# Column halves for the 128x64 products of a triangular inverse, ScalarE copies behind them, and fewer turns of waiting around it

## The chip, the cores and the metric

The kernel runs on one core of a Trainium2 chip. The metric is the time on the device in microseconds (us), the median over runs of the same program. The engines are TensorE (PE in the profile; its weight loads are PEld), VectorE (DVE), ScalarE (ACT), GpSimd (POOL) and SyncE (SP), which issues nearly all DMAs. PSUM has eight banks that TensorE writes and VectorE and ScalarE read.

## The reference

One block of a hybrid decoder, batch 1, 1024 tokens, model width 1024, in float32. After an RMSNorm one projection feeds two groups of heads: eight heads of stick-breaking attention (width 64) and four heads of gated DeltaNet (width 128). Both outputs are normed, gated, projected back and added to the residual; a last RMSNorm follows. What the change touches is the chunked delta rule. There each chunk needs the inverse of a unit lower triangular matrix:

```python
a_mat = jnp.where(strict, jnp.einsum('bhnid,bhnjd->bhnij', k_beta, k) * decay, 0.0)
eye = jnp.eye(CHUNK, dtype=jnp.float32)
rhs = jnp.concatenate([v_beta, k_beta * jnp.exp(g)[..., None]], axis=-1)
sol = lax.linalg.triangular_solve(a_mat + eye, rhs, left_side=True, lower=True,
                                  unit_diagonal=True)
u, w = sol[..., :dv], sol[..., dv:]
```

A scan over the chunks then carries the state of each head. The kernel works with chunks of 128 tokens: eight per head, in two units of four.

## The kernel before

Matrices of the projections are multiplied as three products of rounded parts (high by high, high by low, low by high), which go through TensorE at one pass each; the products of the DeltaNet part are in plain float32 and run as two records each.

**Who sets the order.** The program is written by Python generators, called streams: one for the projections (`projections`, ORDER and LOADS are their order), one for the attention and one per window of it, and for the DeltaNet part `delta_load` (loads of a unit), `delta_pre` (its norms and gram products, `gdn_pre`), `delta_substitute` (`gdn_sub`, which solves 16x16 blocks on POOL), `delta_solve` (`gdn_inv`, the rest of the inverse) and `delta_scan` (`gdn_chain`, the scan). `interleave` gives turns to them. While it writes, a `Model` of the engines runs along: each recorded instruction gets a cost (`cost`), waits for its inputs, and is placed on its engine by priority when the model has it ready; the order found so is what the chip runs. TensorE executes its instructions in the order in which the streams wrote them. A stream gets a turn only when TensorE's list is empty in the model and when the operations that it yielded have ended there and a margin (HOPS, TO_PE, SLACK) has passed. So a `yield` of an operation means: nothing behind it is written before it is done.

`until(name)` yields twice: until a flag stands, and then for the operation that the flag holds. Flags: `l{u}g` the loads of unit u, `p{u}` its gram products, `x{h}` the 16x16 inverses of head h, `i{u}` the finished inverse.

**The inverse.** `gdn_inv(h)` takes the eight chunks of a head together. It loads the 16x16 results in several layouts (nb, xa, xb), makes 32x32 inverses on POOL and VectorE (`times`), writes them to DRAM and loads them again as xc, transposes them on VectorE (wc). Then it has four turns on TensorE: y1 (16 products of 32x32, `nm` by wc), x1 (24 products of 32x32, xc and y1), which give 64x64 inverses, and y2 and x2 (8 products each, 128 rows, 64 columns), which give the lower 64x64 part of the 128x128 inverse `X` (xinv). y2 multiplies `nm` by `wy`; its result goes back into `wy`; x2 multiplies that by `X` and its result is copied into `X`. TensorE can use a part of its array for a small product; which columns it uses follows from the PSUM partitions of the result. Before, all eight results of y2 lie in partitions 64 to 127, and all eight of x2 in 0 to 63, each in one bank.

**What is loaded how.** For the heads 0 and 1 (h < TURNED) a unit's keys and queries are in SBUF already and are turned by TensorE (rows kwf); for the heads 2 and 3 they come as DMAs from gt_s, and ScalarE squares them.

The last stage projects the normed and gated outputs: first the DeltaNet half of all eight token blocks (`products_delta`), then the attention half (`products_attention`). Its inputs pass through `enter_delta`, `enter_attention`, `out_norm` (tiles both and oss) and `split` (tile mmf, on POOL), in slots that the products free again; the results are added in VectorE to the tile xr.

Of the kernel before, what the change touches and what calls it, by code (L numbers as in the profile page):

```python
# [13 lines left out]
AF = mybir.ActivationFunctionType  # L14
# [3 lines left out]
P = 128  # L18
# [13 lines left out]
TURNED = 2  # L32
# [154 lines left out]
class Model:  # L187
# [3 lines left out]
    def __init__(self, engines):  # L191
        self.now, self.events, self.seq = 0.0, [], 0
        self.regions = {}
        self.heads = {e: [] for e in "VAGS"}
        self.busy = {e: False for e in "VAGS"}
        self.order = {e: [] for e in "VAGS"}
        self.pe, self.pe_busy, self.pe_began, self.table, self.dma = [], False, 0.0, None, 0.0
        self.prio, self.pe_rows = 0, 128

        self.held = {"V": 0.0, "G": 0.0}  # L200
        for e, real in engines.items():
            setattr(self, e, Recorder(self, e, real))
# [18 lines left out]
    def record(self, eng, ins, outs, inputs, cost, table):  # L221
        self.seq += 1
        op = Op(eng, ins, cost, self.prio, self.seq, table)
        if eng == "P":
            op.rows = rows(inputs[0])
            op.load = int(np.prod(inputs[0].shape[1:])) * (0.665 if cost == 58 else 0.845)
        deps = {}
        for ap in outs + inputs:
            r = self.regions.get(ap.tensor.name)
            if r is None:  # L230
                continue
            ids = r.ids(ap)
            for n in np.unique(r.writer[ids]):
                if n >= 0:
                    deps[id(r.ops[n])] = r.ops[n]
            if any(ap is o for o in outs):
                r.mark[ids] = True
                keep = []
                for o, rids in r.reads:
                    if o.end is not None and o.end + 500 < self.now:  # L240
                        continue
                    if r.mark[rids].any():
                        deps[id(o)] = o
                    keep.append((o, rids))
                r.reads = keep
                r.mark[ids] = False
                r.writer[ids] = len(r.ops)
                for o in r.before:
                    deps[id(o)] = o
                for q in (r, r.prev):  # L250
                    if q and q.ops and not q.ops[0].begun:
                        q.ops[0].followers.append(op)
                        op.waits += 1
                if r.before and all(o.end is not None and o.end + 500 < self.now for o in r.before):
                    r.before = []
            else:
                for o in r.before:
                    deps[id(o)] = o
                if r.space == "PSUM":
                    for o, _ in r.reads:  # L260
                        if o.eng != eng:
                            deps[id(o)] = o
                        elif not o.begun:
                            o.followers.append(op)
                            op.waits += 1
                r.reads.append((op, ids))
            r.ops.append(op)
        for d in deps.values():
            if d is op or (d.eng == "P" and eng == "P"):
                continue  # L270
            if d.end is None:
                d.users.append(op)
                op.waits += 1
            else:
                op.ready = max(op.ready, d.end + self.hop(d, op))
        if eng == "P":
            self.pe.append(op)
            self.pull()
        elif not op.waits:
            self.at(max(self.now, op.ready), self.arrive, op)  # L280
        return op
# [79 lines left out]
def rows(ap):  # L361

    return next(n for n in (32, 64, 128) if ap.shape[0] <= n)
# [47 lines left out]
def cost(eng, name, args, kw):  # L411

    size = lambda ap: int(np.prod(ap.shape[1:]))
    n = size(args[0])
    if eng == "S":
        run = min(contiguous(args[0]), contiguous(args[1]))
        return max(60, int(np.prod(args[0].shape)) * 4 / run * (7.5 + run / 23.4) / 16)
    if eng == "P":
        if name == "transpose":
            return 58 if args[1].dtype == F32R else 108  # L420
        n = size(args[2])
        if args[2].dtype == F32R:
            return n * 0.448 + 2
        if rows(args[1]) == 32:
            return 45
        return 2 * max(n / 1.2, 20) + 3
    if eng == "A":
        return (51 if args[1].space == "PSUM" else 93) + n / 1.2 + 93 * isinstance(kw.get("scale"), bass.AP) + 100 * ("accum_out" in kw)
    if eng == "G":
        if name == "tensor_tensor" and args[3] == ALU.pow:  # L430
            return 400 + 155 * n
        if name == "tensor_tensor":
            if args[1].tensor.name == args[2].tensor.name or np.prod(args[2].shape[1:]) < n:
                return 145 + 1.66 * n
            return 147 + (1.76 if args[0].tensor.name.startswith("sg") else 2.68 if len(args[0].shape) > 3 else 2.105) * n
        return 127 + 0.912 * n
    if name == "tensor_reduce":
        n = size(args[1])
    if name == "tensor_tensor_scan":
        return 60 + 2.09 * n  # L440
    return (130 if name == "scalar_tensor_tensor" and isinstance(args[2], bass.AP) else 69) + 1.04 * n
# [50 lines left out]
def block(tc, xT_d, x_d, n1_d, wE_d, wQ_d, wC_d, conv_d, alog_d, dtb_d, mixw_d, wo_d, fnw_d, out_d):  # L492
    nc = tc.nc
    ck = Model({"V": nc.vector, "A": nc.scalar, "G": nc.gpsimd, "P": nc.tensor, "S": nc.sync})
    V, A, G, TE, S = ck.V, ck.A, ck.G, ck.P, ck.S

    with ExitStack() as top:
# [163 lines left out]
        for k in range(NK):  # L661
# [6 lines left out]
            for part, u, n in (("w", 0, 1), ("x", 0, 1)) if k else (("x", 0, 2), ("w", 0, 2), ("w", 1, 2), ("x", 1, 2)):  # L668
                size = (T if part == "x" else 512) // n
# [21 lines left out]
            if k:  # L691
                for j in range(8):
                    i, hs = j // 2, slice((j % 2) * 512, (j % 2) * 512 + 512)
# [99 lines left out]
        flags = {}  # L793
# [219 lines left out]
        def until(name):  # L1013
            yield lambda: name in flags
            yield flags[name]


        def delta_pre():
            yield from decays(pre)
            for h in range(GH):  # L1020
                for g in range(2):
                    u = 2 * h + g
                    yield from until(f"l{u}g")
                    yield from gdn_pre(h, g)

        def delta_load():
# [32 lines left out]

        def delta_solve():  # L1060
            for h in range(GH):
                yield from until(f"x{h}")
                yield from gdn_inv(h)
                for g in range(2):
                    flags[f"i{2 * h + g}"] = True
# [11 lines left out]
        def gdn_pre(h, g):  # L1077
# [30 lines left out]
            r = G.tensor_scalar(mr2b, r2b, -1.0, None, ALU.mult)  # L1108
# [3 lines left out]
            qe, nk = qn[:, 0, :], qn[:, 1, :]  # L1112
            G.tensor_tensor(nk, ss[:, 0, :], root, ALU.pow)
            G.tensor_scalar(qe, ss[:, 1, :], EPS * P, None, ALU.mult)
            yield r
            nm = dt
            for i in range(2):
                gpt = pz()
                for j in range(2):
                    c = 2 * i + j  # L1120
                    TE.matmul(gpt[:, j * 256:(j + 1) * 256], kq[:, c, 0, :], kq[:, c, :, :].rearrange("p a t -> p (a t)"),
                              start=True, stop=True)
                gv = gpt.rearrange("p (j a t) -> p j a t", j=2, a=2)
                V.tensor_tensor(at[:, 2 * i:2 * i + 2, :], gv[:, :, 1, :], dt[:, 2 * i:2 * i + 2, :], ALU.mult)
                for j in range(2):
                    c = 2 * i + j
                    r = V.scalar_tensor_tensor(nm[:, c, :], gpt[:, j * 256:j * 256 + P], mr2b[:, c:c + 1], dt[:, c, :], ALU.mult, ALU.mult)
# [21 lines left out]
        def gdn_sub(h):  # L1149
# [3 lines left out]
            bd = dr.tile([32, 32, 32], F32, tag="bd", bufs=2, name="bd")  # L1153
            xd = xds[h % 2]
            for g in range(2):
                yield from until(f"p{2 * h + g}")
                nms.append(gst[h, g]["nm"])
                for b in range(4):
                    bs = slice(32 * b, 32 * b + 32)
                    S.dma_start(bd.rearrange("(g c b) k i -> g c b k i", g=2, b=4)[g, :, b].rearrange("c k i -> k c i"), nms[g][bs, :, bs])  # L1160
# [21 lines left out]
        def gdn_inv(h):  # L1182
# [7 lines left out]
            xa = gd.tile([P, 4, 32], F32, tag="xc", name="xa")  # L1190
            S.dma_start(xa.rearrange("p r i -> p (r i)"), rows)
            xb = gd.tile([P, 16, 16], F32, tag="xb", name="xb")
            yield S.dma_start(xb.rearrange("p k i -> p (k i)"), xe.rearrange("(n u) f -> n (u f)", u=2).unsqueeze(1).to_broadcast([32, 4, 256]))

            def times(dst, left, right):
                for v in range(2):
# [8 lines left out]
            times(xa[:, :, 16:32], yx, xb)  # L1205
            S.dma_start(rows, xa.rearrange("p r i -> p (r i)"))
            xc = gd.tile([P, 8, 32], F32, tag="xc", name="xc")
            yield S.dma_start(xc, xd[0:32768].rearrange("(g c b r i) -> (b r) (g c) i", g=2, c=4, b=4, r=32, i=32))
            wc = gd.tile([P, 8, 32], F32, tag="wc", name="wc")
            r = V.transpose(wc.rearrange("p c i -> p (c i)"), xc.rearrange("p c i -> p (c i)"))  # L1210
            wy = gd.tile([P, 8, 64], F32, tag="br", name="wy")
# [34 lines left out]

            y2p = pz()
            yv2 = y2p.rearrange("p (c i) -> p c i", c=8)
            for c in range(8):
                TE.matmul(yv2[64:128, c, :], nm(c, slice(0, P), slice(64, 128)), wy[:, c, :], start=True, stop=True)  # L1250
            yield A.activation(wy[64:128], yv2[64:128], AF.Copy)
            x2p = pz()
            xv2 = x2p.rearrange("p (c i) -> p c i", c=8)
            for c in range(8):
                TE.matmul(xv2[0:64, c, :], wy[:, c, :], X[:, c, 64:128], start=True, stop=True)
            yield V.tensor_copy(X[0:64, :, 64:128], xv2[0:64])

        def gdn_chain(h, g):
            st = gst[h, g]
# [465 lines left out]
```

## Time and profile before

| | us |
|---|---|
| median of 3 runs | 626.21 (625.37 to 627.15) |
| the profiled execution | 627.9 |
| its span, first to last instruction | 626.2 |
| 360 products pp<-xh,weh of the projections, busy | 145.2 |
| 64 products y2 (pz<-wy,dt), busy | 4.6 |
| 64 products x2 (pz<-xinv,wy), busy | 4.6 |

The counts are those of records, two for each float32 product. All lines but the last carry one line number (L376), since a helper records every operation; so the views are read by tiles. A group is written out<-in by the names of the tiles, and "pz", "pp", "po" and "pc" are PSUM banks. The busy time of a group adds the records that overlap only once, and their mean duration is longer than the step from one to the next, since products are pipelined. Where a rate matters, the starts are compared.

### The profile page before, as it was taken

The page shows a single profiled execution, that of the slowest core. Times are in us where ns is not written, and L with a number is a line of the kernel's source. Part 1 is how long each engine was busy: PE and PEld are TensorE (multiplying, and loading weights), DVE is VectorE, ACT ScalarE, POOL GpSimd, SP SyncE. Part 2 cuts the span into 40 slices and gives each one's busy share as a digit, 9 for nine tenths or more (in the row PEclk, how much of TensorE's full clock was granted, in tenths as well). Part 3 has the DMA queues.
Part 4 walks back from the last instruction along what each step waited for, and adds up shares of the span by engine and source line. Part 5 has one row for each costly group of instructions (what it writes and reads, how often), then busy time and mean ns, then how long its engine had stood idle before and what let it go on. Part 6 is the DMA issues. An engine that isn't in the chain of part 4 may idle for free.

```text
span 626.2 us, 11144 instructions
## 1 busy us (share of the span) xinstructions
PE 615.2 (98%) x3672; PEld 522.7 (83%) x3672; DVE 447.4 (71%) x801; ACT 396.3 (63%) x965; POOL 345.9 (55%) x435
## 2 busy tenths in 40 slices
PE   8999999999999999999999999999999999999995
PEld 7889988998888888887888888888888888877884
DVE  4369983242587788889789797876988865558864
ACT  6755468733776686885768767766778652223553
POOL 0126043936887469685569696493844316325532
PEclk9999999999999999999999999999999999999998
DMA  8967234775227447679547789245444399897622
GB/s 303 358 233 271 99 108 147 237 267 199 90 81 241 145 126 214 156 186 274 166 117 200 178 229 320 67 151 172 117 149 135 103 236 240 297 245 183 160 110 100
DMA packets 162232, 115.98 MB, mean 185 GB/s; under 512 B 95168, under 2 KB 130176, under 8 KB 162176
## 3 DMA queue, kind: packets, MB, share of 16 engines
q1 hardware_dynamic: 161888, 115.09, 61.3%
q8 instruction: 29, 0.48, 0.3%
q14 instruction: 27, 0.22, 0.1%
q10 hardware_dynamic: 288, 0.20, 0.1%
HBM read 78.12 MB, written 37.13 MB: 184 GB/s over the span
## 4 chain that ended last, share of the span: by engine, by line
PE 92%; issue 2%; DVE 2%; ACT 1%; POOL 1%; DMA 0%; POOLq 0%; DVEq 0%; ACTq 0%
PE pp L376 57%; PE pz L376 25%; PE po L376 7%; PE pc L376 3%; DVE cc L376 1%; POOL oss L376 0%; POOL mmf L376 0%; DMA o_s<-oe 0%; DVE pp L376 0%; ACT ahl L376 0%; ACT xinv L376 0%; ACT pz L376 0%; DVE oe L376 0%; DVE xr L376 0%; ACT sgf L376 0%
## 5 line engine op out<-in xcount | busy, mean ns | idle before, releaser
L376 PE MATMUL pp<-xh,weh 128*128 128x512 f32 x360 | 145.2, 403 | 0.0
L376 PE MATMUL pp<-xh,wel 128*128 128x512 f32 x360 | 140.8, 391 | 0.0
L376 PE MATMUL pp<-xl,weh 128*128 128x512 f32 x360 | 140.7, 391 | 0.0
L376 POOL TENSOR_TENSOR sgf<-sgf,cc 128x128 f32<-128x128 f32 (+3 forms) x64 | 77.2, 1209 | 55.7 <-DVE cc L376 51.6
L376 POOL TENSOR_TENSOR wel<-wer,weh 128x512 fp32r<-128x512 f32 x48 | 62.8, 1311 | 60.8 <-ACT weh L376 49.2
L376 PEld LDWEIGHTS pp<-xh,wel 128*128 128x128 f32 x360 | 67.6, 188 | 14.9
L376 PEld LDWEIGHTS pp<-xh,weh 128*128 128x128 f32 x360 | 67.7, 188 | 12.0
L376 PEld LDWEIGHTS pp<-xl,weh 128*128 128x128 f32 x360 | 67.8, 188 | 11.9
L376 DVE TENSOR_TENSOR_SCAN cc<-pz,step 128x384 f32<-128x384 f32 (+2 forms) x64 | 53.3, 843 | 8.1 <-ACT pz L376 7.3
L376 ACT ACTIVATE sgf<-pz,rs 128x384 f32<-128x384 f32 (+3 forms) x96 | 53.6, 590 | 8.6 <-PE pz L376 8.2
L376 DVE TENSOR_TENSOR ahl<-pz,ahl 128x512 fp32r<-128x512 f32 (+1 forms) x80 | 49.4, 627 | 12.9 <-ACT ahl L376 12.4
L376 ACT ACTIVATE pz<-pz,ns 128x384 f32<-128x384 f32 (+3 forms) x96 | 52.2, 572 | 0.0
L376 ACT ACTIVATE ahl<-pz 128x512 fp32r<-128x512 f32 (+1 forms) x80 | 43.2, 557 | 12.5 <-PE pz L376 12.2
L376 PE MATMUL po<-ahl,v2a 128*128 128x512 f32 (+1 forms) x160 | 49.3, 400 | 0.0
L376 PE MATMUL pp<-wo,mmf 128*128 128x512 f32 x192 | 45.3, 393 | 1.0 <-DVE xr L376 1.0
L376 PEld LDWEIGHTS pp<-wo,mmf 128*128 128x128 f32 x192 | 35.6, 188 | 9.5 <-DVE xr L376 1.6
L376 DVE SCALAR_TENSOR_TENSOR pp<-pre,conv,pp 128x512 f32<-128x512 f32 x42 | 31.3, 746 | 17.1 <-ACT pp L376 16.6
L376 POOL TENSOR_TENSOR mmf<-mgf,mmf 128x512 fp32r<-128x512 f32 x16 | 21.5, 1345 | 39.4 <-ACT mmf L376 37.1
L376 PE MATMUL pp<-woh,mmf 128*128 128x512 f32 (+2 forms) x136 | 41.4, 382 | 0.0
L376 DVE TENSOR_TENSOR_SCAN cc<-pz,cc,step 128x512 f32<-128x512 f32 (+1 forms) x32 | 38.5, 1204 | 2.4 <-ACT pz L376 1.5
L376 PE MATMUL pz<-kh,q 128*128 128x384 f32 (+3 forms) x96 | 35.6, 378 | 0.5 <-ACT wy L376 0.3
L376 PEld LDWEIGHTS pz<-step,stf 128*128 128x128 f32 x288 | 30.6, 141 | 5.8 <-POOL sgf L376 0.4
(318 smaller groups left out, 1504.5 us busy)
## 6 DMA issues: line engine op xcount, KB each, us to landing
wer<-wE SPq DMA_DIRECT2D x48, 256.0 KB, 3.5
xr<-x SPq DMA_DIRECT2D x16, 512.0 KB, 6.7
v_s<-v2e SPq DMA_DIRECT2D x16, 256.0 KB, 3.0
v2a<-v_s SPq DMA_DIRECT2D x16, 256.0 KB, 2.9
q<-qk_s SPq DMA_DIRECT2D x8, 512.0 KB, 4.9
kh<-qk_s SPq DMA_DIRECT2D x8, 512.0 KB, 4.8
kl<-qk_s SPq DMA_DIRECT2D x8, 512.0 KB, 6.2
o_s<-oe SPq DMA_DIRECT2D x32, 128.0 KB, 3.3
```

What stands on the lines that cost most here:

```text
L376: ins = f(*args, **kw).ins
```

## The change

It has three parts.

First, y2 and x2: the products of the chunks 4 to 7 write the other half of the partitions (y2 to 0 to 63, x2 to 64 to 127), and the order of the eight alternates between the halves. The results are copied in two ScalarE instructions of 256 columns each, one per half; for x2 they take the place of one VectorE copy of 512.

Second, waits in the writing: `delta_pre`, `delta_solve` and `gdn_sub` wait for flags alone and no longer for the operations behind them (`delta_pre` still does for the heads 0 and 1), `gdn_pre` waits for the loads later, ahead of its gram products, and two yields behind DMAs in `gdn_inv` go.

Third, the planner's numbers: its costs of 32-row products and of products with 64 columns are lower, and a change between array shapes now includes the width.

```diff
-            op.rows = rows(inputs[0])
-            op.load = int(np.prod(inputs[0].shape[1:])) * (0.665 if cost == 58 else 0.845)
+            op.rows = rows(inputs[0]), int(np.prod(inputs[0].shape[1:])) > 64
+            op.load = int(np.prod(inputs[0].shape[1:])) * (0.665 if cost == 58 else 0.45 if cost < 100 else 0.845)
...
         if rows(args[1]) == 32:
-            return 45
-        return 2 * max(n / 1.2, 20) + 3
+            return 32
+        return (1 if size(args[1]) == 64 else 2) * max(n / 1.2, 20) + 3
...
                     u = 2 * h + g
-                    yield from until(f"l{u}g")
+                    yield lambda: f"l{u}g" in flags
+                    if h < TURNED:
+                        yield flags[f"l{u}g"]
                     yield from gdn_pre(h, g)
...
             for h in range(GH):
-                yield from until(f"x{h}")
+                yield lambda: f"x{h}" in flags
                 yield from gdn_inv(h)
...
             G.tensor_scalar(qe, ss[:, 1, :], EPS * P, None, ALU.mult)
-            yield r
+            yield [r] + flags[f"l{2 * h + g}g"]
...
             for g in range(2):
-                yield from until(f"p{2 * h + g}")
+                yield lambda: f"p{2 * h + g}" in flags
                 nms.append(gst[h, g]["nm"])
...
-            yield S.dma_start(xb.rearrange("p k i -> p (k i)"), xe.rearrange("(n u) f -> n (u f)", u=2).unsqueeze(1).to_broadcast([32, 4, 256]))
+            S.dma_start(xb.rearrange("p k i -> p (k i)"), xe.rearrange("(n u) f -> n (u f)", u=2).unsqueeze(1).to_broadcast([32, 4, 256]))
...
-            yield S.dma_start(xc, xd[0:32768].rearrange("(g c b r i) -> (b r) (g c) i", g=2, c=4, b=4, r=32, i=32))
+            S.dma_start(xc, xd[0:32768].rearrange("(g c b r i) -> (b r) (g c) i", g=2, c=4, b=4, r=32, i=32))
...
-            for c in range(8):
-                TE.matmul(yv2[64:128, c, :], nm(c, slice(0, P), slice(64, 128)), wy[:, c, :], start=True, stop=True)
-            yield A.activation(wy[64:128], yv2[64:128], AF.Copy)
+            for c in (0, 4, 1, 5, 2, 6, 3, 7):
+                TE.matmul(yv2[64:128, c, :] if c < 4 else yv2[0:64, c, :], nm(c, slice(0, P), slice(64, 128)), wy[:, c, :], start=True, stop=True)
+            yield [A.activation(wy[64:128, 0:4], yv2[64:128, 0:4], AF.Copy), A.activation(wy[64:128, 4:8], yv2[0:64, 4:8], AF.Copy)]
...
-            for c in range(8):
-                TE.matmul(xv2[0:64, c, :], wy[:, c, :], X[:, c, 64:128], start=True, stop=True)
-            yield V.tensor_copy(X[0:64, :, 64:128], xv2[0:64])
+            for c in (0, 4, 1, 5, 2, 6, 3, 7):
+                TE.matmul(xv2[0:64, c, :] if c < 4 else xv2[64:128, c, :], wy[:, c, :], X[:, c, 64:128], start=True, stop=True)
+            yield [A.activation(X[0:64, 0:4, 64:128], xv2[0:64, 0:4], AF.Copy), A.activation(X[0:64, 4:8, 64:128], xv2[64:128, 4:8], AF.Copy)]
```

No instruction of TensorE is added or removed; the order of nearly all streams against each other is another one, since the planner decides each turn by its own clock. Three places of it follow. Rows are out<-in with the size of the result and a count.

On TensorE, from y2 of head 0 (pz<-wy,dt) to x2 (pz<-xinv,wy), before the change. Around them stand gram products of the next unit (kqf), transposes of its values (vt) and work of the attention (po, stf):

```order
L376 MATMUL pp<-xh,wel 128x512
L376 MATMUL pz<-wy,dt 64x64 x8
L376 MATMUL pz<-kqf_1784 128x256 x4
L376 MATMUL pz<-xinv,wy 64x64 x8
L376 MATMUL pz<-step,vt 128x128 x4
L376 MATMUL po<-ahl,v2a 128x512 x2
```

The same place with the change:

```order
L376 MATMUL pp<-xh,wel 128x512
L376 MATMUL pz<-wy,dt 64x64 x8
L376 MATMUL po<-ahl,v2a 128x512 x2
L376 MATMUL pz<-step,stf_2220 128x128 x3
L376 MATMUL po<-ahl,v2a 128x512 x2
L376 MATMUL pz<-step,stf_2365 128x128 x4
L376 MATMUL pz<-xinv,wy 64x64 x8
L376 MATMUL pz<-kh,q_2213 128x128
```

Between the two turns the gram products are replaced by products and transposes of the attention. In the whole order, y1 of this head (pz<-wc,dt) stands in row 899 of 2424 before and in row 843 of 2423 after.

On ScalarE, around the copy behind y2 of head 0, before (nkv,ss are the squares of the next unit's keys and queries, pre belongs to the convolution of the projections):

```order
L376 ACTIVATE nkv,ss<-pz 128x128 x8
L376 ACTIVATE ahl<-pz 128x2x256
L376 ACTIVATE pre<-step 128x3
L376 ACTIVATE pre<-pp 128x512
L376 ACTIVATE pp<-pre,conv 128x512
L376 ACTIVATE wy<-pz 64x512
```

And with the change, on to the copies behind x2 (xinv):

```order
L376 ACTIVATE nkv<-pz,qn 128x128 x4
L376 ACTIVATE nkv,ss<-pz 128x128 x7
L376 ACTIVATE wy<-pz 64x256 x2
L376 ACTIVATE nkv,ss<-pz 128x128
L376 ACTIVATE ahl<-pz 128x384
L376 ACTIVATE ahl<-pz 128x2x256
L376 ACTIVATE xinv<-pz 64x4x64 x2
```

The copies are two each, and they stand close behind the squares.

On POOL, in the last stage, before the change, from the norms of the attention's blocks 0 and 1 (oss x2) to those of the blocks 2 and 3 (each one oss); mmf are the splits of blocks, in the order of the output products:

```order
L376 TENSOR_TENSOR oss<-oss,half 128x8 x2
L376 TENSOR_TENSOR mmf_6724<-mgf_6624,mmf_6724 128x512
L376 TENSOR_TENSOR mmf_6764<-mgf_6650,mmf_6764 128x512
L376 TENSOR_TENSOR mmf_6785<-mgf_6672,mmf_6785 128x512
L376 TENSOR_TENSOR mmf_6820<-mgf_6684,mmf_6820 128x512
L376 TENSOR_TENSOR mmf_6865<-mgf_6743,mmf_6865 128x512
L376 TENSOR_TENSOR mmf_6909<-mgf_6791,mmf_6909 128x512
L376 TENSOR_TENSOR oss<-oss,half 128x8
L376 TENSOR_TENSOR mmf_6969<-mgf_6813,mmf_6969 128x512
L376 TENSOR_TENSOR oss<-oss,half 128x8
```

With the change:

```order
L376 TENSOR_TENSOR oss<-oss,half 128x8 x2
L376 TENSOR_TENSOR mmf_6743<-mgf_6525,mmf_6743 128x512
L376 TENSOR_TENSOR mmf_6787<-mgf_6543,mmf_6787 128x512
L376 TENSOR_TENSOR mmf_6833<-mgf_6589,mmf_6833 128x512
L376 TENSOR_TENSOR mmf_6882<-mgf_6672,mmf_6882 128x512
L376 TENSOR_TENSOR oss<-oss,half 128x8 x2
L376 TENSOR_TENSOR mmf_6936<-mgf_6769,mmf_6936 128x512
```

Between the two pairs of norms stand four splits in place of six for block 2, and of seven for block 3.

More of the change, by code (lines that the diff above doesn't have):

```diff
@@ L197, in __init__ @@
         self.pe, self.pe_busy, self.pe_began, self.table, self.dma = [], False, 0.0, None, 0.0
-        self.prio, self.pe_rows = 0, 128
+        self.prio, self.pe_rows = 0, (128, True)
         self.held = {"V": 0.0, "G": 0.0}
```

## The prediction

> **What bounds the kernel.** I read the page first, then TensorE's waits, then the timeline around one inverse. On the page the busy shares and the chain that ended last come before all else:
>
> ```profile
> PE 615.2 (98%) x3672; PEld 522.7 (83%) x3672; DVE 447.4 (71%) x801; ACT 396.3 (63%) x965; POOL 345.9 (55%) x435
> PEclk9999999999999999999999999999999999999998
> PE 92%; issue 2%; DVE 2%; ACT 1%; POOL 1%; DMA 0%; POOLq 0%; DVEq 0%; ACTq 0%
> ```
>
> TensorE (PE) is busy in 98% of the span at its full granted clock, and 92% of the last chain is its own work. No stage stands out in which another engine sets the pace. What TensorE lost to others is in the view of waits, for that engine alone (line waited for: total us, times, longest):
>
> ```profile
> PE po L376 <- DVE step L376: 1.7, 1, 1.7
> PE pp L376 <- DVE xr L376: 1.0, 2, 0.8
> PE pz L376 <- DVE cc L376: 0.5, 2, 0.3
> PE pz L376 <- ACT wy L376: 0.3, 1, 0.3
> PE pz L376 <- DVE wy L376: 0.2, 1, 0.2
> ```
>
> The first row is the start of the program, which the change doesn't touch. The other four make 2.0 us. So two things count: TensorE time that goes away counts in full, since some other product is nearly always ready behind it; and all waiting that a better order could remove is about 2.0 us. Moving work of other engines is worth nothing beyond that.
>
> **The products of the inverse.** Per head there are two turns of eight 128x64 products (y2 reads wy, x2 reads wy and writes for xinv). The timeline of head 0 shows both, each product as two records:
>
> ```profile
> 211.76 1.15 PE L376 MATMUL pz<-wy,dt 128*64 128x64 f32 x16
> 212.84 1.99 PE L376 MATMUL pz<-kqf 128*128 128x256 f32 x8
> 214.76 1.15 PE L376 MATMUL pz<-xinv,wy 128*64 128x64 f32 x16
> 215.84 0.53 PE L376 MATMUL pz<-step,vt 128*128 128x128 f32 x4
> ```
>
> A turn keeps TensorE from 211.76 to 212.84 and from 214.76 to 215.84, 1.08 us each. For the beat inside it, the same timeline from the second record on, and the duration of one record in the view by tile:
>
> ```profile
> 211.87 1.04 PE L376 MATMUL pz<-wy,dt 128*64 128x64 f32 x15
> L376 PE MATMUL pz<-wy,dt x64: 222/222/270, 211.8 to 464.3; 128*64 128x64 f32 x64
> ```
>
> Fifteen records take 1.04 us and the last one lasts 0.222, so 14 steps take 0.82: one record starts every 58 ns. All eight use the same half of the array's columns, so none can run beside the next.
>
> The change puts products 4 to 7 into the other half and alternates the halves. Does this chip run two such products at once? The earlier turns of the same inverse tell. In y1 each of eight steps has two 32x32 products, in x1 three:
>
> ```profile
> 205.52 0.69 PE L376 MATMUL pz<-wc,dt 32*32 32x32 f32 x32
> 206.15 0.54 PE L376 MATMUL pz<-step,vt 128*128 128x128 f32 x4
> ...
> 207.82 0.22 PE L376 MATMUL pz<-xc,y 32*32 32x32 f32 x2
> 207.84 0.21 PE L376 MATMUL pz<-y,xc 32*32 32x32 f32 x1
> 207.88 0.20 PE L376 MATMUL pz<-xc,y 32*32 32x32 f32 x2
> 207.89 0.19 PE L376 MATMUL pz<-y,xc 32*32 32x32 f32 x1
> ...
> 208.46 0.54 PE L376 MATMUL pz<-step,stf 128*128 128x128 f32 x4
> ```
>
> 32 records of y1 take 205.52 to 206.15, 0.63 us; 48 records of x1 take 207.82 to 208.46, 0.64 us. Half as many records again cost nothing, and they start in groups of three. The third product of x1 (xc by y1) reads partitions 32 to 63, as one of the other two does, and differs from it in its columns alone. That is the situation of the two halves: same rows, other columns. So I take full overlap: 16 records need eight beats in place of sixteen, 8 x 58 ns = 0.47 us less per turn, and with two turns in each of four heads **3.7 us less**. The bounds: nothing, if the halves exclude each other at this size; and no more than 3.7, since there are only two halves. A loss is excluded because the records keep number and shape, and y1 changes its place in the array with every product at no visible price. The count of changes between array shapes stays the same.
>
> **The copies behind them.** y2 is now emptied by two ScalarE (ACT) copies in place of one, x2 by two on ScalarE in place of one on VectorE (DVE):
>
> ```profile
> 213.21 0.59 ACT L376 ACTIVATE wy<-pz 64x512 f32<-64x512 f32 x1
> 215.94 0.68 DVE L376 COPY xinv<-pz 64x512 f32<-64x512 f32 x1 [0.34 <-PE pz L376]
> L376 ACT ACTIVATE o2f<-po 128x256 f32<-128x256 f32 x32 | 12.3, 386 | 19.6 <-PE po L376 15.9 <-DVE oe L376 2.8 <-PE pz L376 0.9
> ```
>
> A 256-wide copy from PSUM took 386 ns, so two take 0.77: 0.18 us more than 0.59 and 0.09 more than 0.68. Over four heads that is 4 x 0.27 = 1.1 us of added latency. Its cover: between y2 and x2 TensorE does other work. In head 0 the old copy began at 213.21 and two new ones would have ended at 213.98, while x2 started at 214.76, so 0.78 us were spare. In the new order of head 0 the cover is two pairs of attention-value products and seven transposes. Two rows price them:
>
> ```profile
> 292.55 0.73 PE L376 MATMUL po<-ahl,v2a 128*128 128x512 f32 x2
> 293.11 0.37 PE L376 MATMUL pz<-step,stf 128*128 128x128 f32 x3
> 293.32 0.70 PE L376 MATMUL po<-ahl,v2a 128*128 128x512 f32 x2
> ```
>
> Pair to transposes 0.56 us, three transposes 0.21, so some 1.6 us in all with the last four; needed are 0.37 (212.84 to 213.21) and 0.77. It fits with some 0.4 to spare. Seven squares of the next unit stand ahead of the copies on ScalarE, which may use this up; I expect a wait of 0.3 us or less there, about what the rows on wy (0.5 us) show now at other heads. These cancel: **0**. Without cover the price is the 1.1 us; below nothing is not excluded, since the 0.5 us of waits on wy could go: 0.5 less to 1.1 more.
>
> The Trainium skill, page "TensorEngine Tiling (Array Packing)", section "PSUM Bottleneck", speaks against this part: it says to empty PSUM with ScalarE and VectorE both, and to take several tiles in one access, and the change gives both turns to ScalarE and cuts the access in two. By that rule the 1.1 us would show and the sum would be 3.1 instead of 4.2; the 0.78 us of spare time in this trace speaks for the cover.
>
> **The turns that no longer wait.** Loads, products and preparation are written without waiting a turn. No instruction goes; each stands earlier. The first inverse product of head 0 moves from row 899 to row 843 of TensorE's order, the other heads similarly, and the DeltaNet chain ends earlier, so more of the last projections stand behind it. While TensorE is full this gives nothing. It can give something in the tail, where this happened:
>
> ```profile
> 561.69 0.69 DVE L376 TENSOR_TENSOR bothf<-bothf 128x512 f32<-128x512 f32 x1 [2.11 <-DMA bothf<-o_s]
> ...
> 562.97 0.68 DVE L376 TENSOR_TENSOR xr<-pp,xr 128x512 f32<-128x512 f32 x1
> ...
> 563.70 3.04 PE L376 MATMUL pp<-wo,mmf 128*128 128x512 f32 x12 [0.81 <-DVE xr L376]
> ```
>
> VectorE stood 2.11 us before the load of an attention block, the evacuation xr came late behind it, and TensorE waited 0.81 for its bank. This and a second one (0.16) are the 1.0 us of the waits. With the DeltaNet blocks split earlier, POOL reaches the norms of attention blocks 2 and 3 two splits sooner, so these loads should be needed less urgently; but the loads still take turns for slots that the products free. I take half: **0.5 us less**; the bounds are 1.0 less and, by the same kind of wait once more, 1.0 more.
>
> For the rest of the reshuffle I take 0. It can remove the 0.5 us on cc, and what it can add is the rival below.
>
> **The sum.** 3.7 + 0 + 0.5 = 4.2 us less. The profiled execution took 627.9 us, of which 626.2 are the span: 623.7 after it. The median of the runs shown is 626.21, 1.7 under the profiled one; the same cut gives **622.0**.
>
> **Rivals.**
> *The halves take turns.* Then only the 0.5 remains: 625.7. The groups of three in x1 speak against it; for it speaks that no product of 128 rows in two column halves is in this trace. 0.10.
> *The copies show.* If x2 and the chain stand behind ScalarE, 1.1 us come back: 623.1. For it: the seven squares ahead of the copy; against: the spare 0.78. The page named above would have this one. 0.08.
> *An engine now stands before a load, and it ends slower.* Before, a load was waited for in the writing, so its reader was queued late:
>
> ```profile
> 192.82 0.59 SPq L376 DMA_DIRECT2D xc<-xd  x1
> 199.86 0.43 DVE L376 STREAM_TRANSPOSE wc<-xc 128x256 f32<-128x256 f32 x1
> xb<-xe SPq DMA_DIRECT2D x4, 128.0 KB, 3.1
> bothf<-o_s SPq DMA_DIRECT2D x32, 128.0 KB, 4.9
> ```
>
> VectorE transposed xc 7.0 us after its load was issued. 128 KB loads of short runs took 3.1 and 4.9 us to landing (medians). If the transposition is now queued for 3.1 us and the load takes 4.9, VectorE stands 1.8 us, and behind it the scans cc and the parts ahl that TensorE needs: four heads, 7.2 us. If all of it reached TensorE the time would be 629.2; from 4.2 us, 1.05 per head, the gain is gone. Against it: TensorE has windows of attention and projections queued, and today's 2.11 us stand of VectorE cost it only 0.81. By that ratio 7.2 us would cost 2.8 and leave 624.8, with a gain of 1.4. I give the partial form 0.09 and the slower end 0.06.
>
> **How the numbers follow.** Forecast 0.67, the rivals 0.10, 0.08, 0.09 and 0.06. About 0.3% (1.9 us, here 624.3) is what a measurement of this kernel can tell from no change. Faster by more: the forecast and the copies, and a little of the partial form: 0.77. Within: the taking of turns and most of the partial form: 0.16. Slower: 0.07. The range runs from 620.0 (3.7 and all 2.0 us of waits gone make 620.5, with 0.5 for what the view of waits doesn't list) to 625.0, which takes in the shown copies and the partial form; the halves that take turns and the slower end, 0.16, stay out, with a few in a hundred below.
>
> **What will show it.** A y2 and an x2 turn should last about 0.61 us in the timeline in place of 1.08, with records in pairs. If they last 1.08, the first term is wrong. Waits of TensorE on wy and xinv above 0.5 us in all would show the copies. The wait on xr in the tail should be about half. New idle time of VectorE before wc with a load named, or of ScalarE before the squares of heads 2 and 3, would show the third rival. The prediction is wrong if new waits on engines that the reshuffle made late outweigh the 3.7 us.

## The result: slower by 1.3%

The changed kernel took 634.1 us (median of four, 632.41 to 635.17) beside 625.8 for the kernel before: a ratio of 1.0126, 95% interval 1.0098 to 1.0154, some 8 us. The prediction said 622.0. The profiled execution took 633.95 us, its span is 632.1, 5.9 more than before.

On the page after, the lines that answer to those shown of before:

```profile
PE 612.9 (97%) x3672; PEld 520.3 (82%) x3672; DVE 446.5 (71%) x797; ACT 399.7 (63%) x977; POOL 346.2 (55%) x435
PEclk9999999999999999999999989999999999999998
PE 74%; DVE 7%; POOL 5%; DMA 4%; ACT 4%; issue 3%; SPq 3%; POOLq 0%; DVEq 0%; ACTq 0%
```

TensorE is busy for 2.3 us less and the span is longer; its own work makes 74% of the last chain in place of 92%. One slice at full clock has become an 8. What TensorE waited for after the change (line waited for: total us, times, longest):

```profile
PE pz L376 <- DVE ahl L376: 3.1, 3, 2.3
PE pp L376 <- DVE zt L376: 2.6, 1, 2.6
PE po L376 <- DVE step L376: 1.7, 1, 1.7
PE pp L376 <- ACT bothf L376: 1.3, 1, 1.3
PE pz L376 <- DVE xinv L376: 0.9, 2, 0.5
PE pz L376 <- DVE cc L376: 0.8, 3, 0.4
PE pz L376 <- DMA kl<-qk_s: 0.6, 1, 0.6
PE pp L376 <- DVE ac L376: 0.5, 1, 0.5
PE pz L376 <- ACT pz L376: 0.4, 1, 0.4
PE po L376 <- DMA v2a<-v_s: 0.2, 1, 0.2
```

Without the start (step) these are 10.4 us where there were 2.0. The two rows on wy are gone, and so is xr; in their place stand ahl, zt and bothf. The timeline of head 2 shows the turns of y2 and x2:

```profile
366.48 0.69 PE L376 MATMUL pz<-wy,dt 128*64 128x64 f32 x16 [0.55 <-DVE xinv L376]
367.10 0.50 PE L376 MATMUL pp<-xh,weh 128*128 128x512 f32 x1
...
368.69 0.69 PE L376 MATMUL pz<-xinv,wy 128*64 128x64 f32 x16
369.31 0.62 PE L376 MATMUL po<-ahl,v2a 128*128 128x512 f32 x2
```

A turn lasts 0.62 us from its start to the next product's: 0.46 less than before, 3.7 us in eight turns. So the gain came, and other things stand against it.

**The longest two waits.** The first is 2.3 us before 373.68. The timelines of TensorE and of ScalarE around it:

```profile
370.91 0.46 PE L376 MATMUL pc<-nkv,xinv 128*128 128x128 f32 x2
373.68 0.50 PE L376 MATMUL pz<-kh,q 128*128 128x512 f32 x1 [2.32 <-DVE ahl L376]
...
369.48 0.77 ACT L376 ACTIVATE xinv<-pz 64x256 f32<-64x256 f32 x2
370.16 0.30 ACT L376 ACTIVATE akf<-akf 128x128 f32<-128x128 f32 x1
...
371.62 0.29 ACT L376 ACTIVATE akf<-nkv 128x128 f32<-128x128 f32 x1
371.82 0.19 ACT L376 ACTIVATION_READ_ACCUMULATOR akf<-nkv 128x1 f32 x1
372.03 0.38 ACT L376 ACTIVATE o2f<-po 128x256 f32<-128x256 f32 x1
372.31 0.97 ACT L376 ACTIVATE ahl<-pz 128x512 fp32r<-128x512 f32 x2
```

ScalarE isn't idle. It makes the two copies behind x2 (xinv), which the change moved to it and which hold it for 0.68 us. From 370.16 on it squares the next unit's keys and queries (akf), which is not urgent, and the part of the attention (ahl) that VectorE and then TensorE need stands behind all of these in its queue. Some 20 us earlier ScalarE stood idle before such squares: its waits have a row on the load of nkv, which before has not.

```profile
ACT akf L376 <- DMA nkv<-gt_s: 2.7, 1, 2.7
```

The second is 2.6 us at the entry of the last stage. SyncE's timeline, then VectorE and TensorE:

```profile
523.44 7.99 SPq L376 DMA_DIRECT2D bothf<-o_s  x8
531.55 0.54 SPq L376 DMA_DIRECT2D gate_s<-zt  x1
...
534.64 0.69 DVE L376 TENSOR_TENSOR zt<-pp,zs 128x512 f32<-128x512 f32 x1 [1.66 <-DMA gate_s<-zt]
...
535.39 1.88 PE L376 MATMUL pp<-wo,mmf 128*128 128x512 f32 x7 [2.59 <-DVE zt L376]
```

SyncE issues eight loads of attention blocks (bothf) for 8.0 us. The store of zt queues behind them; the next zt needs the slot that this store frees; it reads a PSUM bank (pp), and the next output product waits for the bank.

After the first of the two waits the granted clock fell. In the view by windows (PEclk is the third column from the right), around that wait:

```profile
366.00:371.00 5.00, 4.52 (x52) 3.82 (x53) 3.16 (x5) 3.68 (x16) 2.29 (x3) 1.00 0.78 154
371.40:374.00 2.60, 0.32 (x1) 0.30 (x2) 1.55 (x4) 1.87 (x9) 1.66 (x4) 1.00 0.86 214
374.00:378.00 4.00, 4.00 (x12) 3.15 (x11) 3.23 (x7) 3.90 (x9) 1.16 (x4) 0.57 0.68 217
```

Four us at 0.57 lose another 4 x 0.43 = 1.7 us. The account of the profiled executions: 8.4 us more waiting, 1.7 of low clock, 3.7 less work: 6.4 more, against 5.9 measured.

### The profile page after: what moved, and what is told of

Same layout as the page of the kernel before. It is cut to its first block, busy times and chain, and to the rows that moved or that the text cites. A ratio compares the mean times of both kernels' runs of the same rounds, so it can differ in the third digit from the quotient of the medians.

```text
span 632.1 us, 11172 instructions
## 1 busy us (share of the span) xinstructions
PE 612.9 (97%) x3672; PEld 520.3 (82%) x3672; DVE 446.5 (71%) x797; ACT 399.7 (63%) x977; POOL 346.2 (55%) x435
## 4 chain that ended last, share of the span: by engine, by line
PE 74%; DVE 7%; POOL 5%; DMA 4%; ACT 4%; issue 3%; SPq 3%; POOLq 0%; DVEq 0%; ACTq 0%
PE pp L376 44%; PE pz L376 21%; PE po L376 6%; PE pc L376 3%; SPq L376 3%; DVE cc L376 1%; DMA nkv<-gt_s 1%; POOL wel L376 1%; POOL tt L376 1%; DMA worf<-wo 1%; POOL kqf L376 1%; DVE ahl L376 1%; DMA v2a<-v_s 1%; DMA q<-qk_s 1%; DMA gate_s<-zt 0%
## 5 line engine op out<-in xcount | busy, mean ns | idle before, releaser
L376 ACT ACTIVATE weh<-wer 128x512 fp32r<-128x512 f32 x48 | 30.3, 636 | 11.2 <-DMA wer<-wE 6.2
```

What stands on the lines that cost most here:

```text
L376: ins = f(*args, **kw).ins
```

## The experiments

Theory at the start: **the order costs it** (the halves are worth their 3.7 us, the new order takes some 12). Rivals: the halves or their copies cost it; and within the order, the removed waits, the planner's numbers, or any reshuffle at all. Ratios are to the kernel before on the same chip.

### The halves with the order held still

Two kernels separate the first part of the change from the order. In the first, the halves stand in before's own order: the planner is told the cost of the old single copy for the first of two and nothing for the second, so that every engine's order is that of before, but for the copies that are now two.

```diff
+            FOLD[:] = [0, 51 + 512 / 1.2]
+            yield [A.activation(wy[64:128, 0:4], yv2[64:128, 0:4], AF.Copy), A.activation(wy[64:128, 4:8], yv2[0:64, 4:8], AF.Copy)]
...
+            FOLD[:] = [0, 69 + 1.04 * 512]
+            yield [V.tensor_copy(X[0:64, 0:4, 64:128], xv2[0:64, 0:4]), V.tensor_copy(X[0:64, 4:8, 64:128], xv2[64:128, 4:8])]
```

> Only the column halves of y2 and x2, with the copies on their old engines (two of 256 columns each) and every instruction of every engine in the order of before. Theory 'the order costs it' (the halves are worth 3.6 us and what was lost lies in the new order): 3.0 to 3.7 us under before, about 622.3. Rival 'the halves or their copies cost it' (two copies where one was, halves that disturb what runs beside them): within 1 us of before, or above it.

In the second, after's order is kept on every engine and the halves are undone; the copies, not shown, read where the products now write.

```diff
-                TE.matmul(yv2[64:128, c, :] if c < 4 else yv2[0:64, c, :], nm(c, slice(0, P), slice(64, 128)), wy[:, c, :], start=True, stop=True)
+                TE.matmul(yv2[64:128, c, :], nm(c, slice(0, P), slice(64, 128)), wy[:, c, :], start=True, stop=True)
...
-                TE.matmul(xv2[0:64, c, :] if c < 4 else xv2[64:128, c, :], wy[:, c, :], X[:, c, 64:128], start=True, stop=True)
+                TE.matmul(xv2[0:64, c, :], wy[:, c, :], X[:, c, 64:128], start=True, stop=True)
```

> The changed kernel with every instruction in its own order and its ScalarE copies, but all eight products of a turn write the same partitions again. Theory 'the order costs it': the turns last 1.08 us again, 3 to 4 us over after, about 637.5, so the order alone costs 11 to 12 us against before. Rival 'the halves cost it': at or under after, 626 to 634.

The halves in the old order took 0.9949 of before (0.9929 to 0.9970), 3.2 us less, as expected; its turns last 0.62 us. Without them the new order took 1.0141 (1.0099 to 1.0184), 8.9 us more. So the rival falls: the halves with two copies a turn gain 3.2 us, and the order loses what is lost. In the first kernel the copies behind x2 are still VectorE's; no run shows by itself what moving them to ScalarE does. That the second kernel is only 1 us above after, not 3 to 4, was not expected; the intervals overlap too far to tell.

### The two parts that move the order

Only the removed waits (all the yields of the diff, nothing else), and only the planner's numbers (the five lines of `Model` and `cost`).

> Only the second part of the change: the waits that the writing no longer makes, with the products, copies and planner numbers of before. Theory 'the removed waits cost it' (readers queued ahead of their loads): 634 to 638. Rival 'the planner's numbers cost it': 625 to 628. Third theory, 'any new order costs some, by chance': somewhere in 627 to 633.

> Only the third part of the change, the planner's numbers, with the products, copies and waits of before. Theory 'the removed waits cost it': 625 to 628. Rival 'the planner's numbers cost it': 634 to 638. Third theory, 'any new order costs some, by chance': 627 to 633.

Waits alone: 1.0142 (1.0106 to 1.0178), 8.9 us more. Numbers alone: 1.0099 (1.0070 to 1.0129), 6.2 us more. Each alone costs most of the loss, so neither is the cause by itself, and they don't add. In the trace with the waits alone TensorE's waits without the start make 10.2 us where before has 2.0, spread over a dozen rows of which none is above 1.8 us. What the numbers lose is in the main one place again, at the entry of the last stage. SyncE, VectorE and TensorE there:

```profile
519.10 8.50 SPq L376 DMA_DIRECT2D bothf<-o_s  x6
...
529.83 2.48 SPq L376 DMA_DIRECT2D xr<-x  x4
...
535.80 1.29 DVE L376 TENSOR_TENSOR xr<-pp,xr 128x512 f32<-128x512 f32 x2 [1.13 <-DMA xr<-x]
...
536.64 9.60 PE L376 MATMUL pp<-wo,mmf 128*128 128x512 f32 x34 [4.05 <-DVE xr L376]
```

Again the bothf loads take SyncE, for 8.5 us, here ahead of the loads of xr. VectorE can't add the first output product to xr, its bank stays full, and TensorE stands 4.05 us. In before the first output product starts at 526.23; six such loads are issued 14 us ahead of it, and xr 4 us ahead:

```profile
511.86 7.17 SPq L376 DMA_DIRECT2D bothf<-o_s  x6
...
522.28 1.54 SPq L376 DMA_DIRECT2D xr<-x  x3
```

### Controls: another order for no reason

To see what a reshuffle costs as such, one planner number is off by 1 ns, and by 5; nothing else changes.

```diff
-            return 45
+            return 46
```

> A control: before with one planner number off by a nanosecond (a 32-row product is costed at 46 in place of 45), and nothing else. The order is that of before up to about the middle of TensorE's row and another one behind it. Theory 'any new order costs some' (the order of before is a lucky one): 2 to 8 us over before. Rival 'only the removed waits and the changed numbers cost it': within 1.5 us of before.

> A second control of the same kind: a 32-row product costed at 40 in place of 45. Theory 'any new order costs some': 2 to 8 us over before, by stalls at places that differ from the first control's. Rival 'only the removed waits and the changed numbers cost it': within 1.5 us of before.

They took 1.0083 (1.0055 to 1.0111) and 1.0050 (1.0021 to 1.0080): 5.2 and 3.1 us more. The first control's order on TensorE is that of before up to 297 us of 626, and a nanosecond in the planner costs two thirds of what the change lost. TensorE's waits in it:

```profile
PE pp L376 <- DVE xr L376: 2.3, 1, 2.3
PE po L376 <- DVE step L376: 1.7, 1, 1.7
PE pz L376 <- DVE ahl L376: 1.1, 2, 0.6
PE pz L376 <- DVE y L376: 0.9, 1, 0.9
PE pz L376 <- DVE cc L376: 0.6, 2, 0.4
PE pz L376 <- ACT wy L376: 0.3, 1, 0.3
PE pz L376 <- DVE wy L376: 0.2, 1, 0.2
```

The longest is the wait on xr at the entry of the last stage, where before has none. So the 2.0 us of waiting of before is a property of its order, not of the program.

### Single waits put back

After with all its waits back, and after with the load wait alone back (the lines of `delta_pre` and `gdn_pre`, shown here).

```diff
-                    yield lambda: f"l{u}g" in flags
-                    if h < TURNED:
-                        yield flags[f"l{u}g"]
+                    yield from until(f"l{u}g")
...
-            yield [r] + flags[f"l{2 * h + g}g"]
+            yield r
```

> The changed kernel with all its waits back (halves, ScalarE copies and planner numbers stay). Theory 'the removed waits cost it': 622 to 624, faster than before. Theory 'any new order costs some': the halves' 3.6 us less and some 3 to 8 us more, 625 to 631, so at or above before and below after.

> The changed kernel with one wait back: the gram products and ScalarE squares of a unit are written only when its loads have landed, as before. TensorE's order is that of after up to row 1037 and another one behind it. Theory 'the squares of heads 2 and 3 queued before their loads cost it': the stalls of after at 348 to 378 us (6 us with the lower clock behind them) go, so 627 to 629. Theory 'any new order costs some': these go and others come, 630 to 638, no better than after by more than 2 us.

All back: 1.0033 (1.0012 to 1.0054), 2.1 us over before and some 6 under after, as the theory of any new order had it; the removed waits are not the whole. The load wait back: 1.0063 (1.0034 to 1.0092), 4.0 us over before, some 4 under after, between the two expectations. Its trace has no row of ScalarE on the nkv load any more, the 2.3 us on ahl are gone and the clock stays up, but a new wait of 1.5 us on cc has come.

### The loads of bothf written later

Four kernels hold back the writing of these loads until the last projection and the first load of xr are written.

```diff
-            yield lambda: f"e{SBH - 1}3" in flags and fx.room("sg3")
+            yield lambda: f"e{SBH - 1}3" in flags and fx.room("sg3") and "proj" in flags and 0 in xs_
```

> The kernel with the planner's numbers alone, and one gate more: the loads of the attention blocks (bothf from o_s) are written only after the last projection and the first load of xr. All that stands before the last stage keeps its place. Theory 'the issue of these loads on SyncE holds up what the last stage needs first': the stall of 4.2 us at 532 us and the some 1.8 us of lower clock behind it go, 5 to 6 us less than that kernel had, so within 1.5 us of before. Rival 'the stall is the order of VectorE and stays, or comes back at another place': within 2 us of 633 (5 us over before).

> The changed kernel with the same gate. Theory 'the issue of these loads holds up the stores of zt': the stall of 2.8 us at 532 us goes and that at 578 us stays or shrinks, 2.5 to 4 us less than after, 3.5 to 5.5 us over before. The stalls of 348 to 378 us stay. Rival 'comes back elsewhere': 7 to 9 us over before, as after.

> The first control (one planner number off by a nanosecond) with the same gate. Theory: its stall of 2.5 us at 534 us and the lower clock behind it (1.6 us) go, 3.5 to 4.5 us less than the control, 0.5 to 2 us over before. Rival: 4 to 6 us over before, as the control.

> The column halves in the order of before, with the same gate; there the loads stood ahead of the last stage already and cost nothing. Theory: within 1 us of the halves alone, 3 to 4 us under before. Rival 'the later loads are missed in the attention half of the last stage': 1 to 4 us slower than the halves alone.

After with the gate: 1.0072 (1.0043 to 1.0102), 4.5 us over before, 3.4 less than after, though its ten runs lie as far apart as 628.8 and 637.0. Its TensorE waits have no row on zt or bothf, 0.5 us on xr, and still the 2.3 us on ahl. That is what the theory asked for. With the numbers and in the control it doesn't hold. With the numbers: 1.0102 (1.0070 to 1.0135), as without the gate. There the gate failed to do its work: SyncE's queue has the loads ahead of xr still.

```profile
525.99 4.89 SPq L376 DMA_DIRECT2D bothf<-o_s  x6
531.05 1.39 SPq L376 DMA_DIRECT2D xr<-x  x3
```

In the first control: 1.0113 (1.0077 to 1.0149), not better than the 1.0083 without. There the loads do stand behind xr. The wait on xr is gone, and a new one stands 18 us later, 2.0 us on the splits (mmf, ScalarE). The halves in the old order: 0.9952 (0.9929 to 0.9975), as without the gate.

### Both repairs, and the halves in another order

After with load wait and gate; after with all waits and gate; and the halves in the second control's order, held as in the first experiment.

> The changed kernel with both repairs: the load wait of the units back, and the loads of bothf written late. If the two are separate causes they add: after was 1.0126 of before, the load wait gave 0.6% and the gate 0.5%, so 0.999 to 1.004, about 628. Rival 'stalls only move, the sum stays': 1.006 or more, 631 and above.

> The changed kernel with all its waits back and the gate (halves, copies and numbers stay). Its stall of 2.4 us at 531 us and the 1.6 us of lower clock behind it go if the gate's theory holds here: 0.997 to 1.000 of before, 625 to 627. Rival 'the first xr stands behind the same loads anyway, or the stall moves to 550 us, as in the control': 1.002 to 1.006.

> The second control's order (a 32-row product costed at 40), word for word on every engine, with the column halves of y2 and x2 and copies on their old engines. Theory 'the halves are worth the same in any order': 3 to 3.7 us less than that control, 0.999 to 1.001 of before. Rival 'in an order that already waits for other engines part of the gain is waited away' (as the changed order seems to do, 1.0141 without and 1.0126 with the halves): 1.002 to 1.005.

Both repairs: 1.0044 (1.0026 to 1.0061), 2.8 us over before, 5 less than after. The load wait alone gave some 4 and the gate alone 3.4, each of these differences uncertain by some 2.5 us. Added, they would leave 1.0009, uncertain by 0.005, so whether they add isn't shown. All waits and gate: 1.0086 (1.0066 to 1.0107), worse than without the gate (1.0033): the wait at the entry is gone, and TensorE stands 4.2 us at 546 us instead, with the clock at a half for 6.8 us behind it.

```profile
PE pp L376 <- ACT mmf L376: 4.2, 1, 4.2
```

So here the rival holds, and a stall moved. The halves in the second control's order took 1.0034 (1.0022 to 1.0046), against 1.0050 without: 1.0 us less, not 3.2. The control's own interval is too wide to tell these two apart. The profiled executions show what can happen to a lead. The last stage begins 1.9 us sooner with the halves; then come these rows, of the control, of the kernel with the halves, and of its view by windows:

```profile
535.39 24.73 PE L376 MATMUL pp<-wo,mmf 128*128 128x512 f32 x108 [1.75 <-DVE xr L376]
...
533.71 26.20 PE L376 MATMUL pp<-wo,mmf 128*128 128x512 f32 x108 [2.53 <-DVE xr L376]
...
533.38:536.79 3.41, 3.08 (x7) 2.51 (x8) 0.78 (x2) 0.15 (x1) 1.27 (x1) 0.50 0.96 274
```

The wait on xr has grown from 1.75 to 2.53 us, so part of the lead is waited away. Behind the longer wait the clock stood at 0.50 for 3.41 us, which the control's trace doesn't have, and the same 108 products last 26.20 us in place of 24.73. Of a lead of 1.7 us at the start of these rows 0.2 is left at their end.

**The version that beats both** is the halves in the old order: 624.7 us beside 628.0 for the kernel before on that chip.

## Why the prediction was wrong

- **What bounds the kernel.** Right that TensorE time counts in full, in this order. "All waiting that a better order could remove is about 2.0 us" is a bound on the gain alone. I let it stand for both sides. Of the kernels with another order from the middle of the program on, or from further ahead, none was as fast as before, and a nanosecond's difference in the planner cost 5.2 us.
- **The products, 3.7 us.** Right: 0.62 us a turn where 0.61 was forecast, and 3.2 us in the time where the order is held.
- **The copies, 0.** Right as far as TensorE's waits go: none on the ScalarE copies is listed after the change, the 0.5 us on wy are gone, and the two waits on xinv (0.32 and 0.55 us) stand before y2 and are for VectorE's copies. The Trainium skill, page "TensorEngine Tiling (Array Packing)", section "PSUM Bottleneck", advises to empty PSUM with ScalarE and VectorE both. The 1.1 us that the prediction worked out for this rule did not show among TensorE's waits. But the sum looked only at y2 and x2. The copies behind x2 also hold ScalarE for 0.68 us ahead of the longest wait; what that cost is not shown.
- **The turns that no longer wait, 0.5 less.** Wrong in sign. The 1.0 us on xr did go, but zt (2.6 us) and bothf (1.3 us) came in the same stage. That loads "should be needed less urgently" looked at POOL's order of splits; what decided the wait on zt was SyncE's, where eight issues of 1.0 us on average stood before a store.
- **"For the rest of the reshuffle I take 0."** This is the step that failed: a term put at nothing with no row behind it. In after the new waits of 8.4 us and the 1.7 us of low clock outweigh the 3.7 us. Removed waits alone cost 8.9 us, new numbers alone 6.2, a nanosecond in the planner 5.2, five nanoseconds 3.1. The new orders that were run without halves and without repairs cost 3 to 9 us, not 0.
- **The third rival** had the right kind and the wrong place. I put the price on VectorE before the transposes of xc; VectorE's idle time before them names no load after the change. What was queued too early were ScalarE's squares, which the list of signs named but the sum did not price, and SyncE's loads. Its slower end, 629.2, took one engine at one place per head. Putting the load wait back, which also reorders what follows, gave some 4 us, about half of the loss; the gate on the bothf loads gave 3.4, and both together 5, each uncertain by 2 to 3 us. The 2.8 us that stay over before, which with the halves' 3.2 make some 6 us of loss, were not separated further.

## What to carry to other kernels

When an order is decided by a planner's clock, a change that touches its numbers or yields has the price of a reshuffle; measure that price by a control that changes one number by nothing that matters, and hold the order still to see what the edit itself is worth. A list of short waits says what may be gained, never what may be lost. Before a yield behind a load goes, look at each engine that will then queue the reader, and at the DMA-issuing queue: a long run of issues for data that is needed late can hold up the load or store that the next product waits for. Moving such a run is itself a new order, to be measured: it gained 3.4 us in the changed order, and in two others the stall moved elsewhere and nothing was gained.

## What the runs showed of the hardware

A wait of some 2.5 us can cost more than itself. In the kernel with the numbers alone the granted clock after its 4.05 us wait was 0.61, over 4.4 us (a loss of 1.7):

```profile
537.00:541.40 4.40, 4.40 (x14) 3.45 (x13) 0.39 (x2) 0.00 (x0) 0.64 (x1) 0.61 0.74 204
```

But after the 2.59 us wait at 532 us in after it stayed at 1.00, and in after with the gate it stayed up behind the very wait on ahl (2.3 us, with the same products around it) that was followed by 0.57 in after.

What differs is the place of the wait on a grid of time. Each fall of the clock in the middle of these runs went to 0.50 and lasted 3.41 us, but for one of twice that. In after the clock came back at 377.60 and fell next at 626.77, when TensorE's work was done: 73 times 3.413 us. So the view by windows can be cut on that grid. The first three rows are after; the others are after with the gate, counted back from the fall at 624.65 behind its last product:

```profile
367.36:370.77 3.41, 3.41 (x34) 2.75 (x33) 1.86 (x3) 3.29 (x15) 1.09 (x1) 1.00 0.82 146
370.77:374.18 3.41, 1.09 (x8) 0.85 (x7) 1.73 (x5) 2.68 (x13) 1.76 (x5) 1.00 0.89 196
374.18:377.59 3.41, 3.41 (x10) 2.68 (x9) 2.64 (x6) 3.41 (x8) 0.65 (x3) 0.50 0.68 222
...
368.65:372.06 3.41, 2.10 (x20) 1.82 (x15) 0.59 (x3) 3.33 (x18) 0.87 (x3) 1.00 0.88 158
372.07:375.48 3.41, 2.40 (x11) 2.04 (x12) 2.92 (x7) 3.06 (x9) 1.65 (x5) 1.00 0.60 182
375.48:378.89 3.41, 3.41 (x18) 2.88 (x17) 3.41 (x7) 2.96 (x8) 1.32 (x1) 1.00 1.01 320
```

In after one step of the grid holds the whole wait: TensorE (second number) is busy for 1.09 of 3.41 us, and the next step runs at 0.50. With the gate the same wait lies across two steps, busy for 2.10 and 2.40 us, and no step runs low. The 2.59 us wait in after is cut into steps with 1.60 and 2.63 us busy. No sharp limit follows: with the waits alone a step with 1.71 us busy was followed by 0.50.

The Trainium skill, page "TensorE: Matmul & The Clock Gate", section "Part 1: The HAM clock gate", has the clock fall after an idle window of about 3.4 us, where the window runs freely. The length and the free running agree with these traces; that the whole window has to be idle does not, since 2.3 us of idle in one step was enough here.
